# A third of the weight differences computed on GpSimd beside the modulation sums, and the gates' rows fetched through ScalarE's queue

## The chip, the core and the metric

One core of one Trainium2 chip runs the whole program. The metric is the device time of one launch in microseconds (us). Five engines work side by side and meet through semaphores: PE (TensorE, matmuls, with PEld for its weight loads), DVE (VectorE), ACT (ScalarE), POOL (GpSimd) and SP (SyncE, which here only issues transfers). Each engine takes its instructions strictly in the order in which they stand in its own queue. An instruction that waits holds up everything behind it on its engine.

## What is computed

Two layers of a diffusion trunk, for 256 latent tokens and 256 context tokens, width 1024, all in float32. The shift, scale and gate vectors ("modulation") of a layer are one long matrix-vector product of the conditioning vector with `w_ada` (1024 x 9216 for each layer).

```python
def swiglu(h, w1, w2):
    a, b = jnp.split(h @ w1, 2, axis=-1)          # 1024 -> 2 x 2816
    return (jax.nn.silu(a) * b) @ w2              # 2816 -> 1024

for layer in range(2):
    m = jnp.split(silu(c) @ w_ada[layer] + b_ada[layer], 9, axis=-1)   # and the same for the context
    x = sandwich_out(x, swiglu(sandwich_in(x, m, 0, g[0]), w1[layer, 0], w2[layer, 0]), m, 0, g[1], 0.5)
    x = sandwich_out(x, token_mixing(sandwich_in(x, m, 1, g[2]), ...), m, 1, g[3], 1.0)
    x = sandwich_out(x, swiglu(sandwich_in(x, m, 2, g[4]), w1[layer, 1], w2[layer, 1]), m, 2, g[5], 0.5)

def sandwich_in(x, mods, idx, g):       # norm, then scale and shift
    return rms_norm(x, g) * (1 + mods[3 * idx + 1]) + mods[3 * idx]
def sandwich_out(x, y, mods, idx, g, w):    # gate on the way back
    return x + w * mods[3 * idx + 2] * rms_norm(y, g)
```

There are four SwiGLU blocks ("FFN" below). The first three work on all 512 tokens, the last one on the 256 latent tokens alone.

## The kernel before

**Split products.** PE multiplies in a reduced float32 form (fp32r). To keep the precision, each operand is held as two blocks: `hi`, the value rounded to fp32r, and `lo`, the difference between the value and `hi`. A product is three matmuls: hi times hi, lo times hi, hi times lo (L92 is the line of all of them). Activations live in HH and HL, the hidden values of an FFN in nine pairs of blocks inside R.

**A weight unit.** Weights come in units of 128 x 1024 values (512 KB). The class `Unit` loads one into one of four raw buffers (raw0 to raw3) by a transfer on SP's queue (L183). Its method `parts` then makes the two blocks: ScalarE casts the raw values to `hi` (L190), and VectorE subtracts (`raw - hi`, L195) to make `lo`. Both go into a slot, one of the w or R tiles, and eight slots serve the units of an FFN in turn. The raw buffer is free for the next transfer when `lo` is done. Which engine subtracts is the unit's field `lo_eng`, V (VectorE) by default.

**Modulation beside the FFN.** While PE works on the FFN of one stage, VectorE computes modulation vectors that a later stage needs (`ada_v`): units of `w_ada` come through the same four raw buffers, and for each one VectorE does four multiply-adds of 128 x 512 (L486, L488) into two running sums in the tile sx. PE then adds the partitions up, and for a gate vector `gate_done` (L461, L462) adds a bias row, multiplies by a gain row and stores the gate to DRAM (L463, on ScalarE's queue). The bias and gain rows are fetched by `gate_rows` (L453, L454): eight transfers of 2 KB for a gate, four for each half of it, 48 in all, issued by SP among the weight units. They go into two sets of tiles, (grow, grow) and (rstd, rstd). Sixteen vectors are left for the first three FFNs, six in the first and five in each of the others; all six gates are among them.

**Order.** The kernel writes down a list of steps with planned times (`schedule`), then walks it once (`run`). At each step `run` first issues the loads that have a free buffer, then makes the parts of those units that are due: a unit is due when its first use is at most `LOOK` = 2.5 us of planned time away, or when its data should be there. The units come in the order of their first use. Behind this the recording layer may still swap neighbours in an engine's queue.

**An FFN** (`ffn`) goes through 22 columns of hidden blocks in three chunks. `pair` makes one hidden block from two units of w1, `chunk` multiplies a chunk's blocks by units of w2 and adds the result to the tile YB: ScalarE copies it for the first chunk (L683), VectorE adds it for the second (L685), and the third is the tail. The banks that these instructions empty are needed at once by the matmuls of the other half of the chunk.

Of the kernel before, what the change touches and what calls it, by code (L numbers as in the profile page):

```python
# [17 lines left out]
D = 1024  # L18
# [4 lines left out]
T = SEQ + CTX  # L23
# [56 lines left out]
def hybrid_trunk(ctx: ExitStack, tc, x, c, ctx_in, c_ctx, w_ada, b_ada, norm_g, ffn_w1, ffn_w2, w_in, w_out,  # L80
                 na_rpb, pool_w, pool_scale, diff_lambda, diff_subln_g, const, out):
    nc = tc.nc
    V, S, G = nc.vector, nc.scalar, nc.gpsimd
# [80 lines left out]
    def lo_engine(n):  # L164

        turn[0] += 1
        return G if n and turn[0] % n == 0 else V
# [63 lines left out]
    prog = []  # L231
# [40 lines left out]
    DMA_US, DMA_LAT, LOOK = 1.46, KN['dlat'], KN['look']  # L272

    def run():
        seq = []
        for i, st in enumerate(prog):
            for u in st.units:
                if u.first is None:
                    u.first = i
                    seq.append(u)  # L280
                u.last = i
        owner = {}
        for u in seq:
            if u.split:
                sl = min(u.slots, key=lambda z: owner[z].last if z in owner else -1)
                u.slot, u.prev = sl, owner.get(sl)
                owner[sl] = u
        mark = {st.mark: i for i, st in enumerate(prog) if getattr(st, "mark", None)}
        nl = ns = 0
        dma = 0.0  # L290

        ring = []

        def can_load(i):
            if nl >= len(seq) or mark.get(seq[nl].gate, -1) > i:
                return False
            if seq[nl].own is not None:
                p = seq[nl].own_prev
                return p is None or p.last < i
            if len(ring) < len(raws):  # L300
                return True
            o = ring[-len(raws)]
            return hasattr(o, "hi") if o.split else o.last < i

        def can_split(i):
            if ns >= nl:
                return False
            u = seq[ns]
            if not u.split:
                return True  # L310
            if isinstance(u.after, str) and mark[u.after] > i:
                return False
            return u.prev is None or u.prev.last < i

        for i, st in enumerate(prog):
            t = st.t - st.dur
            extra = 1
            while True:
                if can_load(i):
                    u = seq[nl]  # L320
                    if u.own is None:
                        u.load(raws[len(ring) % len(raws)])
                        ring.append(u)
                    else:
                        u.load(u.own)
                    dma = max(dma, t) + DMA_US
                    u.there = dma + DMA_LAT
                    nl += 1
                    continue
                if can_split(i):  # L330
                    u = seq[ns]
                    must = prog[u.first].t - prog[u.first].dur <= t + LOOK
                    if not u.split:
                        ns += 1
                        continue
                    if must or (u.there <= t and extra > 0):
                        u.parts(SLOTS[u.slot])
                        extra -= 0 if must else 1
                        ns += 1
                        continue  # L340
                break
            assert all(u.first > i or hasattr(u, "hi") or not u.split for u in st.units), i
            st.fn()
# [101 lines left out]
    def gate_set(h):  # L445
        return RSTD if h else (GROW[:, 1], GROW[:, 2])

    def gate_rows(l, j, h):

        bias, gain = gate_set(h)  # L450
        for v in range(2):
            rs = slice(64 * v, 64 * v + 64, 32)
            nc.sync.dma_start(out=bias[rs], in_=b_ada[l, j * D + h * T : j * D + (h + 1) * T].rearrange("(f c) -> f c", f=2))  # L453
            nc.sync.dma_start(out=gain[rs], in_=norm_g[l, 2 * (j // 3) + 1, h * T : (h + 1) * T].rearrange("(f c) -> f c", f=2))  # L454

    def gate_done(l, j, h):

# [12 lines left out]
    def ada_v(l, *js):  # L470

        st = []
        for j in js:
            for h in range(2):
                box = {}
                for q in range(4):
                    if q == 2 and j % 3 == 2:
                        st.append(Step(lambda l=l, j=j, h=h: gate_rows(l, j, h)))
                    u = Unit(w_ada[l, q * SEQ : (q + 1) * SEQ, j * D + h * T : j * D + (h + 1) * T], split=False)

                    def fn(u=u, q=q):
                        for z in range(2):
                            for v in range(2):
                                sv = sc[:, 2 * q + z, v : v + 1]
                                if q == 0 and z == 0:
                                    V.tensor_scalar(out=ACC[v], in0=u.raw[:, z, :], scalar1=sv, scalar2=None, op0=ALU.mult)  # L486
                                else:
                                    V.scalar_tensor_tensor(out=ACC[v], in0=u.raw[:, z, :], scalar=sv, in1=ACC[v], op0=ALU.mult, op1=ALU.add)  # L488

                    st.append(Step(fn, [u]))  # L490
# [123 lines left out]
    def ffn(l, f, groups, done=0):  # L614
# [4 lines left out]
        both = len(groups) == 2  # L619
        allc = ALLC if both else GROUPS[groups[0]]  # L620
        ring = tuple(range(8))

        def unit(src, lo=V):
            u = Unit(src, slots=ring, lo=lo)
            u.after = f"ffn{l}{f}"
            return u

# [11 lines left out]
        def w1_units(j):  # L639
            a, b = [lo_engine(KN["fmod"] if j < (KN["front"] if l == 0 or f == 0 else KN["lf"]) else 0) for _ in range(2)]  # L640
            return unit(w1[:, j * P : (j + 1) * P], a), unit(w1[:, DFF + j * P : DFF + (j + 1) * P], b)
# [60 lines left out]

        nf = 0 if done or not both else FRONT
        fr = [w1_units(j) for j in range(nf)]
        for j in range(nf):
            for u in fr[j]:
                u.hi_v = j < KN["hv"] if not both else j < KN["hb"] if f else j < KN["hc"]
# [73 lines left out]
        end = Step(lambda: None)  # L781
        end.mark = f"tail{l}{f}"
        body.append(end)
        for u in lu[1:]:
            u.after, u.tail = end.mark, True
        al = range(j0, j1)
        tail = {LAT: tail_of(2, lu, banks[0:2], al) + tail_of(3, lu, banks[2:4], al)}
        c0, c1 = [(banks[4:6], banks[0:2])[t] for t in range(2)]
# [536 lines left out]
    both = (LAT, CTXG)  # L1325
# [56 lines left out]
    def marked(name):  # L1382
        s = Step(lambda: None)
        s.mark = name
        return s

    f = ffn(0, 0, both, PAIRS)
    raw_u = [GTB[:, 0], GTB[:, 1], SX[:, :D]]
    w1f = ffn_w1[0, 0].rearrange("(k p) (h n) -> k p h n", p=P, h=2)
# [41 lines left out]
    for l in range(DEPTH):  # L1431
# [4 lines left out]
        for g, h in ((LAT, hl), (CTXG, hc)):  # L1436
            front[g][0].needs += h[:2]
            front[g][2].needs += h
        schedule(tail[LAT] + tail[CTXG] + [marked(f"mix{l}")] + wait_h(front[LAT], hl) + wait_h(front[CTXG], hc), hl + hc)
        f = ffn(l, 1, (LAT,) if last else both)  # L1440
        main.insert(len(main) // 2, Step(lambda l=l: gate_load(l, 1, (LAT,) if l else both)))
        if last:
# [15 lines left out]
        else:  # L1458
# [13 lines left out]
            tail = nf[2]  # L1472

    run()


# [23 lines left out]
```

## Time and profile before

| | us |
|---|---|
| three timed runs | 1788.02, 1788.70, 1781.35 |
| their median | 1788.02 |
| the profiled execution, whole time | 1785.39 |
| its span, first to last instruction | 1783.6 |
| PE busy in the span | 1731.2 (97%) |
| DVE busy | 1149.2 (64%) |
| ACT busy | 702.9 (39%) |
| POOL busy | 79.1 (4%) |

The first FFN runs from about 20 to 400 us of the span, the token mixing of layer 0 to about 690, the second FFN to 1015, the third to 1390, the mixing of layer 1 to about 1620, and the fourth FFN to the end. In the table PE's share says where to look, not how close PE is to its peak: what tells is the list of PE's waits, and how many matmuls a stretch holds. On DVE, ACT and POOL a busy time is the engine's own work; waits at the head of a queue are not in it.

### The profile page before, as it was taken

To read this page: it belongs to the slowest core of one execution; us is meant where nothing else is said; L and a number is where in the kernel's file an instruction comes from. 1 tells how busy PE (TensorE), PEld (TensorE's weight loads), DVE (VectorE), ACT (ScalarE), POOL (GpSimd) and SP (SyncE) were. 2 spreads that over 40 slices of the span, in tenths; PEclk is the share of its full clock that TensorE was granted. 3 is DMA by queue.
4 is the path that set the end of the run, shared out by engine and by line. 5 is a ranking of instruction groups with operands and counts; after the bars stand their busy time and mean duration, and the time that the engine had idled before them with its cause. 6 is when DMAs were issued, how large, how long until landed. Compare 5 with 4: busy or idle time off the path is not lost.

```text
span 1783.6 us, 23841 instructions
## 1 busy us (share of the span) xinstructions
PE 1731.2 (97%) x9281; PEld 1438.0 (81%) x9281; DVE 1149.2 (64%) x1804; ACT 702.9 (39%) x1224; POOL 79.1 (4%) x130
## 2 busy tenths in 40 slices
PE   6899999999999999999999999999999999979998
PEld 3687787778977789788788798888887898768997
DVE  4757767766368774666766576576765647865553
ACT  4323222235377753332222452233123536754442
POOL 0000000001000410000000000000000100300000
PEclk9999999999999999999999999999999999989999
DMA  9737546645111232565655434555555331337661
GB/s 283 226 118 215 175 143 197 180 133 137 55 53 48 85 95 84 158 197 155 188 154 165 128 109 153 154 154 177 166 153 164 98 92 60 110 116 227 185 189 60
DMA packets 292096, 255.96 MB, mean 144 GB/s; under 512 B 16128, under 2 KB 236048, under 8 KB 291984
## 3 DMA queue, kind: packets, MB, share of 16 engines
q1 hardware_dynamic: 290176, 253.48, 47.7%
q8 instruction: 72, 1.18, 0.3%
q10 hardware_dynamic: 1808, 0.97, 0.2%
q14 instruction: 40, 0.33, 0.1%
HBM read 253.32 MB, written 1.10 MB: 143 GB/s over the span
## 4 chain that ended last, share of the span: by engine, by line
PE 80%; DMA 8%; DVE 6%; ACT 4%; issue 2%; SPq 0%; ACTq 0%; POOL 0%; DVEq 0%; POOLq 0%
PE bank L92 78%; DMA raw<-in_ffn_w_dram 6%; DVE R L195 1%; DVE sx L488 1%; ACT R L190 1%; PE bank L882 1%; DVE w L195 1%; ACT w L190 1%; PE bank L560 1%; DMA raw<-in_w_ada_dram 1%; DMA gtb<-in_w_ada_dram 1%; ACT YB L867 0%; DMA sil<-in_b_ada_dram 0%; DVE R L376 0%; DVE sil L634 0%
## 5 line engine op out<-in xcount | busy, mean ns | idle before, releaser
L92 PE MATMUL bank<-HH,R 128*128 128x512 f32 (+1 forms) x1932 | 511.4, 349 | 4.6 <-ACT HH L1362 3.5
L92 PE MATMUL bank<-HH,w 128*128 128x512 f32 (+1 forms) x1508 | 424.2, 360 | 0.0
L92 PEld LDWEIGHTS bank<-HH,R 128*128 128x128 f32 x1932 | 339.8, 190 | 56.6 <-issue 6.6
L92 PE MATMUL bank<-R 128*128 128x512 f32 (+3 forms) x1728 | 380.1, 377 | 2.2 <-ACT R L1101 0.9
L92 PEld LDWEIGHTS bank<-R 128*128 128x128 f32 (+1 forms) x1728 | 293.0, 188 | 73.0 <-issue 6.7
L92 PE MATMUL bank<-HL,R 128*128 128x512 f32 (+1 forms) x966 | 334.6, 346 | 0.0
L195 DVE TENSOR_TENSOR R<-raw,R 128x1024 fp32r<-128x1024 f32 (+1 forms) x182 | 221.0, 1219 | 151.4 <-ACT R L190 151.1
L488 DVE SCALAR_TENSOR_TENSOR sx<-raw,sc,sx 128x512 f32<-128x512 f32 x448 | 309.9, 747 | 12.9 <-DMA raw<-in_w_ada_dram 12.7
L190 ACT CAST R<-raw 128x1024 fp32r<-128x1024 f32 (+1 forms) x182 | 189.3, 1045 | 317.4 <-DMA raw<-in_ffn_w_dram 221.1
L92 PEld LDWEIGHTS bank<-HH,w 128*128 128x128 f32 x1508 | 268.2, 190 | 47.6 <-issue 9.6
L195 DVE TENSOR_TENSOR w<-raw,w 128x1024 fp32r<-128x1024 f32 (+1 forms) x140 | 171.4, 1226 | 152.0 <-ACT w L190 150.3
L92 PE MATMUL bank<-HL,w 128*128 128x512 f32 (+1 forms) x754 | 268.3, 356 | 0.0
L190 ACT CAST w<-raw 128x1024 fp32r<-128x1024 f32 (+1 forms) x140 | 146.1, 1047 | 233.5 <-DMA raw<-in_ffn_w_dram 160.5
L92 PE MATMUL bank<-w,R 128*128 128x512 f32 x864 | 210.5, 394 | 6.2 <-DVE YB L685 2.2
L92 PEld LDWEIGHTS bank<-HL,R 128*128 128x128 f32 x966 | 183.2, 190 | 22.5 <-DVE HL L1363 0.2
L92 PEld LDWEIGHTS bank<-w,R 128*128 128x128 f32 x864 | 159.5, 188 | 43.8 <-issue 3.2
L92 PEld LDWEIGHTS bank<-HL,w 128*128 128x128 f32 x754 | 143.2, 190 | 19.1 <-issue 0.7
L636 ACT CAST R<-sil 128x512 fp32r<-128x512 f32 (+1 forms) x92 | 49.7, 540 | 158.5 <-DVE sil L634 158.3
L634 DVE TENSOR_TENSOR sil<-sil,bank 128x512 f32<-128x512 f32 (+1 forms) x92 | 53.9, 586 | 89.2 <-PE bank L92 88.8
L530 POOL TENSOR_TENSOR sr<-sr,eps 128x1 f32<-128x1 f32 x42 | 29.0, 692 | 1426.0 <-DVE sr L529 1426.0
L633 ACT ACTIVATE sil<-bank 128x512 f32<-128x512 f32 (+1 forms) x92 | 47.4, 516 | 81.4 <-PE bank L92 77.5
L637 DVE TENSOR_TENSOR R<-sil,R 128x512 fp32r<-128x512 f32 (+1 forms) x92 | 54.2, 590 | 18.4 <-ACT R L636 18.0
(163 smaller groups left out, 1245.6 us busy)
## 6 DMA issues: line engine op xcount, KB each, us to landing
raw<-in_ffn_w_dram SPq DMA_DIRECT2D x258, 512.0 KB
raw<-in_w_ada_dram SPq DMA_DIRECT2D x128, 512.0 KB
raw<-in_w_in_dram SPq DMA_DIRECT2D x40, 512.0 KB
raw<-in_w_out_dram SPq DMA_DIRECT2D x16, 512.0 KB
gtb<-in_w_ada_dram SPq DMA_DIRECT2D x20, 256.0 KB
gtb<-gate SPq DMA_DIRECT2D x10, 512.0 KB
raw<-in_ffn_w_dram SPq DMA_DIRECT2D x8, 384.0 KB
sx<-in_w_ada_dram SPq DMA_DIRECT2D x8, 256.0 KB
```

The lines of the kernel that those rows point to most:

```text
L92: tab["mm"] = nc.tensor.matmul(out=o, lhsT=l, rhs=r, start=start, stop=stop)
L190: ins = S.copy(out=self.hi, in_=self.raw)
L195: ins = self.lo_eng.tensor_tensor(out=self.lo, in0=self.raw, in1=self.hi.bitcast(F32), op=ALU.subtract)
L488: V.scalar_tensor_tensor(out=ACC[v], in0=u.raw[:, z, :], scalar=sv, in1=ACC[v], op0=ALU.mult, op1=ALU.add)
L530: G.tensor_tensor(out=a, in0=a, in1=mhalf, op=ALU.pow)
L560: ins = nc.tensor.transpose(out=pt[:, z, t * P : (t + 1) * P], in_=y[:, t, k * P : (k + 1) * P], identity=ident)
L633: S.activation(out=sl[:, cs], in_=oa, func=AF.Silu)
L634: V.tensor_tensor(out=sl[:, cs], in0=sl[:, cs], in1=ob, op=ALU.mult)
L636: tab["hs"] = S.copy(out=uh[:, cs], in_=sl[:, cs])
L637: tab["hv"] = V.tensor_tensor(out=ul[:, cs], in0=sl[:, cs], in1=uh[:, cs].bitcast(F32), op=ALU.subtract)
L882: nc.tensor.transpose(out=bv[:, n, i * P : (i + 1) * P], in_=e[:, i * nk + n * P : i * nk + (n + 1) * P], identity=ident)
```

## The change

Four edits. (1) In `ffn`, `unit` counts its calls, and in the three FFNs that work on all tokens every third unit gets `lo_eng = G`: GpSimd does its subtraction. (2) The units of the first four columns of an FFN, whose subtraction stands at the hand-over from the stage before, and those of the tail are set back to VectorE. (3) In `run` a unit of GpSimd is due 3.5 us of planned time earlier than the others. (4) `gate_rows` issues its transfers on ScalarE's queue in place of SP's.

```diff
@@ run @@
-                    must = prog[u.first].t - prog[u.first].dur <= t + LOOK
+                    must = prog[u.first].t - prog[u.first].dur <= t + LOOK + (3.5 if u.lo_eng is G else 0.0)
@@ gate_rows @@
-            nc.sync.dma_start(out=bias[rs], in_=b_ada[l, j * D + h * T : j * D + (h + 1) * T].rearrange("(f c) -> f c", f=2))
-            nc.sync.dma_start(out=gain[rs], in_=norm_g[l, 2 * (j // 3) + 1, h * T : (h + 1) * T].rearrange("(f c) -> f c", f=2))
+            nc.scalar.dma_start(out=bias[rs], in_=b_ada[l, j * D + h * T : j * D + (h + 1) * T].rearrange("(f c) -> f c", f=2))
+            nc.scalar.dma_start(out=gain[rs], in_=norm_g[l, 2 * (j // 3) + 1, h * T : (h + 1) * T].rearrange("(f c) -> f c", f=2))
@@ ffn @@
+        asked = [0]
 
         def unit(src, lo=V):
             u = Unit(src, slots=ring, lo=lo)
+            asked[0] += 1
+            if both and asked[0] % 3 == 0:
+                u.lo_eng = G
             u.after = f"ffn{l}{f}"
             return u
@@ ffn, the first four columns @@
         fr = [w1_units(j) for j in range(nf)]
+        for u in sum(fr, ()):
+            u.lo_eng = V
@@ ffn, the tail @@
         for u in lu[1:]:
-            u.after, u.tail = end.mark, True
+            u.after, u.tail, u.lo_eng = end.mark, True, V
```

What this makes of the engines' queues, at three places. On POOL, between the square roots of the start (L530) and those of the end of the first FFN, before:

```order
L530 TENSOR_TENSOR sr_83<-sr_83,eps 128x1 x2
L530 TENSOR_TENSOR sr_84<-sr_84,eps 128x1 x2
L530 TENSOR_TENSOR sr_85<-sr_85,eps 128x1 x2
L530 TENSOR_TENSOR sr_86<-sr_86,eps 128x1 x2
L905 MEMSET YB 128x384
```

and with the change:

```order
L530 TENSOR_TENSOR sr_84<-sr_84,eps 128x1 x2
L195 TENSOR_TENSOR w_74<-raw_68,w_74 128x1024
L195 TENSOR_TENSOR R<-raw_71,R 128x1024
L195 TENSOR_TENSOR w_72<-raw_68,w_72 128x1024
L195 TENSOR_TENSOR R<-raw_68,R 128x1024
L195 TENSOR_TENSOR R<-raw_70,R 128x1024
L195 TENSOR_TENSOR w_73<-raw_70,w_73 128x1024
```

Seventeen subtractions stand between the two pairs of square roots in the first FFN, and seventeen in each of the next two: 51 of the 322 that VectorE did.

On DVE, late in the first FFN (about 243 to 258 us of the span before; R and w are slots, raw_68 to raw_71 the four raw buffers, sx the running sums), before:

```order
L195 TENSOR_TENSOR R<-raw_69,R 128x1024
L488 SCALAR_TENSOR_TENSOR sx<-raw_68,sc,sx 128x512 x2
L195 TENSOR_TENSOR w_72<-raw_71,w_72 128x1024
L195 TENSOR_TENSOR w_73<-raw_69,w_73 128x1024
L634 TENSOR_TENSOR sil_75<-sil_75,bank_102 128x512
L637 TENSOR_TENSOR R<-sil_75,R 128x512
L195 TENSOR_TENSOR R<-raw_69,R 128x1024
L486 TENSOR_SCALAR sx<-raw_70,sc 128x512 x2
```

and with the change (line numbers of the changed file, six or four higher behind the edits):

```order
L195 TENSOR_TENSOR R<-raw_69,R 128x1024
L195 TENSOR_TENSOR w_73<-raw_69,w_73 128x1024
L638 TENSOR_TENSOR sil_75<-sil_75,bank_102 128x512
L641 TENSOR_TENSOR R<-sil_75,R 128x512
L486 TENSOR_SCALAR sx<-raw_70,sc 128x512 x2
```

Two subtractions have left VectorE's queue here, the one into w_72 and the second one into R. A multiply-add on raw_68 has moved by a place, and the rest stands as it stood.

On ACT, at the start (junk and sr are the sums of squares of the first norm, L1322; the copies to rows, L1339, carry the first modulation sums on to PE), before:

```order
L1322 ACTIVATE junk,sr_83<-X 128x512
L1312 ACTIVATE sil_75<-sil_75 16x128
L1322 ACTIVATE junk,sr_83<-X 128x512 x3
L1339 COPY rows<-bank_105 128x256
L1322 ACTIVATE junk,sr_84<-X 128x512 x4
L190 CAST w_72<-raw_70 128x768
```

and with the change:

```order
L1328 ACTIVATE junk,sr_83<-X 128x512
L453 DMA grow<-in_b_ada_dram 2x256
L1328 ACTIVATE junk,sr_83<-X 128x512
L454 DMA grow<-in_norm_g_dram 2x256
L1328 ACTIVATE junk,sr_83<-X 128x512
L453 DMA grow<-in_b_ada_dram 2x256
L454 DMA grow<-in_norm_g_dram 2x256
L453 DMA rstd_91<-in_b_ada_dram 2x256
L454 DMA rstd_92<-in_norm_g_dram 2x256
L453 DMA rstd_91<-in_b_ada_dram 2x256
L1345 COPY rows<-bank_105 128x256
L454 DMA rstd_92<-in_norm_g_dram 2x256
```

The eight row transfers of the first gate now stand around the first copy to rows. On SP they stood behind the start, among the weight units of the first FFN. The casts L190 keep their places among ScalarE's other instructions, but for some swaps of neighbours.

## Rows read from the trace of the kernel before

**Rows 1.** The page's first part: busy time, share of the span, instructions.

```profile
PE 1731.2 (97%) x9281; PEld 1438.0 (81%) x9281; DVE 1149.2 (64%) x1804; ACT 702.9 (39%) x1224; POOL 79.1 (4%) x130
```

**Rows 2.** Windows: stretch and length, busy us (instructions) per engine, clock, DMA.

```profile
56.00:58.00 2.00, 1.72 (x5) 1.43 (x6) 1.60 (x3) 0.50 (x2) 0.00 (x0) 0.54 1.06 350
...
200.00:250.00 50.00, 50.00 (x232) 40.11 (x231) 32.76 (x55) 10.91 (x15) 0.00 (x0) 1.00 0.49 150
...
750.00:800.00 50.00, 48.10 (x222) 38.30 (x221) 28.59 (x38) 17.00 (x23) 0.00 (x0) 1.00 0.65 185
```

**Rows 3.** PE's waits: instruction, what ended the wait, us in total, times, longest.

```profile
PE bank L92 <- ACT HH L1362: 3.5, 1, 3.5
...
PE bank L92 <- DVE YB L685: 2.2, 2, 1.8
PE bank L92 <- ACT YB L683: 2.1, 2, 1.9
...
PE bank L92 <- DVE s L1361: 1.1, 1, 1.1
...
PE bank L92 <- ACT w L190: 1.1, 1, 1.1
```

**Rows 4.** The page's groups: VectorE's subtractions, mean ns, idle before them and why.

```profile
L195 DVE TENSOR_TENSOR R<-raw,R 128x1024 fp32r<-128x1024 f32 (+1 forms) x182 | 221.0, 1219 | 151.4 <-ACT R L190 151.1
...
L195 DVE TENSOR_TENSOR w<-raw,w 128x1024 fp32r<-128x1024 f32 (+1 forms) x140 | 171.4, 1226 | 152.0 <-ACT w L190 150.3
```

**Rows 5.** Timeline of POOL in the first mixing: start, duration, instruction.

```profile
588.24 1.25 POOL L945 TENSOR_TENSOR YB<-YB,cst 128x8 f32<-128x8 f32 x1
...
591.06 0.73 POOL L949 TENSOR_TENSOR sx<-YB 128x256 f32<-128x256 f32 x1
591.86 2.24 POOL L930 TENSOR_TENSOR YB<-YB 128x271 f32<-128x271 f32 x2
...
594.83 0.20 POOL L945 TENSOR_TENSOR YB<-YB,cst 128x8 f32<-128x8 f32 x1
```

**Rows 6.** Timeline of DVE at the same place.

```profile
591.16 1.71 DVE L195 TENSOR_TENSOR R<-raw,R 128x1024 fp32r<-128x1024 f32 x1 [0.34 <-ACT R L190]
```

**Rows 7.** Timelines of DVE and PE: a subtraction and its first use.

```profile
971.47 1.22 DVE L195 TENSOR_TENSOR w<-raw,w 128x1024 fp32r<-128x1024 f32 x1
...
976.81 0.62 PE L92 MATMUL bank<-HH,w 128*128 128x512 f32 x2
```

**Rows 8.** Timelines of DVE, SP and PE around a chunk's end in the second FFN.

```profile
744.27 0.69 DVE L637 TENSOR_TENSOR R<-sil,R 128x512 fp32r<-128x512 f32 x1
744.87 0.75 DVE L488 SCALAR_TENSOR_TENSOR sx<-raw,sc,sx 128x512 f32<-128x512 f32 x1
745.53 1.22 DVE L195 TENSOR_TENSOR w<-raw,w 128x1024 fp32r<-128x1024 f32 x1
746.67 2.07 DVE L488 SCALAR_TENSOR_TENSOR sx<-raw,sc,sx 128x512 f32<-128x512 f32 x3
748.65 1.22 DVE L195 TENSOR_TENSOR R<-raw,R 128x1024 fp32r<-128x1024 f32 x1
...
748.77 7.63 SPq L183 DMA_DIRECT2D raw<-in_ffn_w_dram  x3
...
756.97 2.37 PE L92 MATMUL bank<-w,R 128*128 128x512 f32 x9 [1.90 <-ACT YB L683]
```

**Rows 9.** Issues by line: count, ns (min/median/max), first and last start.

```profile
L453 SPq DMA_DIRECT2D grow<-in_b_ada_dram x12: 472/481/606, 60.9 to 1170.4; - x12
...
L463 ACTq DMA_DIRECT2D gate<-grow x12: 487/498/618, 119.3 to 1362.7; - x12
```

**Rows 10.** Timelines of ACT, DVE and PE in the start.

```profile
11.96 0.37 ACT L1339 COPY rows<-bank 128x256 f32<-128x256 f32 x1 [3.78 <-PE bank L92]
...
16.17 0.75 DVE L1323 TENSOR_SCALAR YB<-X,sr 128x1024 f32<-128x1024 f32 x1 [0.66 <-POOL sr L530]
...
21.38 1.06 PE L1359 MATMUL bank<-cst,YB 128*128 128x128 f32 x4
```

## The prediction, made before the changed kernel ran

> **What bounds the kernel now.** I read the busy shares first, then the matmul count in windows, then PE's waits. PE is busy for 97% of the span [rows 1]. That alone proves little, so the windows matter: a 50 us stretch in the middle of an FFN holds 232 matmuls at the full granted clock [rows 2], one in 0.216 us, and the stretch with the worst wait among the bodies of the first three FFNs still holds 222 [rows 2]. So there PE runs without gaps nearly everywhere. The list of its waits says how much is left [rows 3]: in the bodies of these FFNs, where the change works, PE waits 2.2 us for additions into YB on VectorE (L685) and 2.1 us for copies into YB on ScalarE (L683); at a tail there is one wait of 1.1 us for a cast. In the start it waits 3.5 us for a cast to HH and 1.1 us for VectorE's s. All five together are 10.0 us, 0.56% of the span. The change takes nothing out of PE's own work. So its gain can be no more than about these 10 us, while a loss has no such ceiling. VectorE, at 64% [rows 1], is no bound; it is idle for 303 us ahead of its 322 subtractions, nearly all of it waiting for ScalarE's cast [rows 4].
>
> **The subtractions themselves.** 51 of 322 leave VectorE. At 1.22 us each [rows 4] that is 62 us of its busy time, all of it beside PE's work. On GpSimd such a subtraction does not occur in the trace. The nearest rows are a two-input instruction over 256 columns, 0.73 us, and one over 8 columns, 0.20 us [rows 5]: (0.73 - 0.20) / 248 = 2.1 ns a column, so an estimate of 0.20 + 1016 x 0.00214 = 2.4 us for 1024 columns. The bounds are 1.22 us, VectorE's own time, and 4 x 0.73 = 2.9 us. I take 2.4, since the two short rows already show how the time grows with the columns. Who waits for it? I followed each of the 51 units from the end of its subtraction to the first matmul that reads it. The smallest distance is 4.12 us: the subtraction that begins at 971.47 and takes 1.22, read at 976.81 [rows 7]. The other fifty lie between 4.6 and 38 us, with a median of about 15. A subtraction that takes 1.2 us more, and starts up to 1.2 us later behind one of VectorE's, ends before its use everywhere. **Price at PE: 0.**
>
> **What GpSimd's work does to VectorE.** In the mixing the two engines run side by side, and the rows show that they take turns. VectorE's subtraction at 591.16 took 1.71 us in place of 1.22 while GpSimd's instruction of 591.06 ran until 591.79 [rows 5, 6]; in return, two additions on GpSimd that follow at 591.86 took 2.24 us together, and an instruction of 8 columns took 1.25 us at 588.24 against 0.20 at 594.83 [rows 5]. So each engine's two-input instruction waits until the other's is over. VectorE gets back about 1.14 us for each subtraction moved (the spacing of its starts, 745.53 to 746.67 [rows 8]) and may lose 2.4 us of standing still. Over 51 units that is between -58 us and +64 us of VectorE's time, in an engine with 36% to spare. PE sees it only where VectorE is late already.
>
> The Trainium skill states the same as a rule against this kind of change: in "SBUF — State Buffer", section "Who interferes with whom", a VectorE instruction with two SBUF inputs and a GpSimd instruction that reads SBUF exclude each other, and the second to issue blocks fully until the first is over. By that rule VectorE stands still whenever it has such work, and the sum would be the slower rival's below; the trace agrees on the mechanism (1.71 us against 1.22), while how often the two meet in an FFN no row of this case shows.
>
> **Where VectorE is late already.** Three places in the three bodies carry waits for emptied banks of more than 0.3 us: two of VectorE's (2.2 us in all) and one of ScalarE's (1.90 of its 2.1).
> - At 757 us PE waits 1.90 us for ScalarE's copy [rows 8]. That copy stands behind casts whose loads SP issued from 748.77 on, as the raw buffers came free. Ahead of this VectorE works without a gap from 744.27 to 749.88, and two of its subtractions there, 745.53 and 748.65, go to GpSimd [rows 8]. They give back 2 x 1.14 = 2.3 us and may block 2 x 2.4 = 4.8 us, since every other instruction in this stretch has two SBUF inputs. So between -1.9 (the wait goes) and +2.5. I take +2, because here VectorE has work queued at every moment.
> - At 275 us the 1.8 us wait [rows 3] stands behind a subtraction that stays on VectorE, whose load came late. The one two units ahead goes to GpSimd. Between -1.8 and +1.2; I take -0.5.
> - At 888 us it is 0.4 us. I take 0.
>
> **Sum for the bodies: +1.5 us, between -4 and +4.**
>
> **The start.** The first unit for GpSimd is the one whose late cast makes PE wait 3.5 us [rows 3]. The cast stays where it is, so the wait stays, and with it the lower clock behind it: 0.54 granted in the 2 us after PE stood still, between the levels of 1.2 and 2.4 GHz [rows 2]. The difference HL for the next matmuls has two SBUF inputs and now meets GpSimd's first subtraction, up to 2.4 us minus the 1.14 that VectorE saves. Against that, one transpose for a later block moves ahead in PE's queue, which can save the 1.1 us wait for s [rows 3], while four of the next block move behind eighteen matmuls. I take +0.5, between -1.1 and +3.
>
> **The row transfers.** SP loses 48 issues of 0.48 us, 23 us; ScalarE gains 48 of about 0.50, the time that its own issue of a gate takes [rows 9], 24 us in an engine that is 39% busy [rows 1]. What queues behind them: casts and the silu of the next hidden block. Each batch of four waits for VectorE's two instructions of the gate before; ScalarE already waits for the second of them at L463, a few instructions later, so little is new. In the start eight issues, 8 x 0.50 = 4.0 us, stand around the first copy to rows, where ScalarE is idle for 3.78 us [rows 10], and one of them waits for the landing of an earlier one. If ScalarE comes 2 us late there, the norm's YB, done at 16.92, comes 2 us later and is read by PE at 21.38 [rows 10]: 4.5 us of cover. **Price: 0**; were the cover gone, up to +4. SP's gain is worth nothing by itself, since its loads wait for raw buffers, which come free by the subtractions.
>
> **The longer look-ahead** moves next to nothing: in ScalarE's queue the casts keep their places but for swaps of neighbours, since most units are made as soon as their data is there. 0.
>
> **The sum.** 1785.4 + 0 + 1.5 + 0.5 + 0 + 0 = 1787.4 us against the profiled execution, 0.1% more. That execution lies 2.6 us under the median of the three runs, which themselves spread over 7 us; so I say **1788.0**, no change. What a measurement of this kernel can tell from no change is about 0.5%, 9 us.
>
> **Rivals.**
> 1. *Faster, VectorE's queue is freed.* A subtraction on VectorE waits at the head of its queue for a cast, and the modulation sums behind it wait too: 303 us of idle time for 322 units [rows 4], so some 48 us for 51. With these on GpSimd the sums go on, raw buffers come free sooner, loads start sooner, and PE's waits for late loads and late copies go. For it speaks the size of this idle time; against it, that ScalarE's casts still stand in one queue, and that PE has only 10.0 us of waits to give [rows 3]. If all go: 1785.4 - 10.0 = 1775.4 us.
> 2. *Slower, VectorE and GpSimd block each other.* It decides where loads run just ahead of their use: about 231 to 275, 680 to 757 and 850 to 888 us, which hold 11 of the 51 units. If each blocks VectorE for its whole length, raw buffers come free 11 x (2.4 - 1.14) = 14 us later in all, and PE gets it in full: 1799 us. For it, [rows 5, 6] and the gapless stretch of [rows 8]; against it, VectorE's idle time and the distances of 4.12 us and more. It takes over once a subtraction on GpSimd ends more than 1.22 + 4.12 = 5.3 us after its cast.
> 3. *Slower, ScalarE is held up by the rows.* Each batch of four costs it 2.0 us, ahead of a silu or a cast. If six of the twelve batches fall on a chunk's end, where PE waits for ScalarE's copies, 6 x 2.0 = 12 us: 1797 us. Against it: of twelve chunk halves' ends only three show a wait of over 0.3 us today.
> That the change doesn't do what it says is no rival: the queues hold 51 subtractions on POOL and 48 row transfers on ACT.
>
> **Chances.** No change, within 9 us of the median: 0.73. Rival 1, faster by more: 0.10. Rival 2: 0.12 and rival 3: 0.05, together slower 0.17. The range takes in the bounds above and part of the rivals: from 1778.5 (rival 1 nearly whole) to 1799 (rival 2).
>
> **What would show it.** The forecast: POOL's subtractions at about 2.4 us, some of them 3 to 4; VectorE's two-input rows stretched beside them; VectorE's busy time down by less than 62 us; PE's matmul count in 200 to 250 us still 232, and its waits for YB within 2 us of today's. Rival 1: those waits gone, and less idle time ahead of L195 by far more than 48 us. Rival 2: new PE waits on POOL's R and w, or longer ones at the chunk ends. Rival 3: ACT's queue waiting at L453 and L454 just ahead of copies to YB, or the start's transposes at 21.38 later. I am wrong if a subtraction on GpSimd takes over 5 us, or if PE's waits outside the start and the three bodies change.

## The result, and the profile with the change

The change is slower: 1812.3 us (median of four runs, 1810.3 to 1814.9) against 1787.6, a ratio of 1.0151 with a 95% interval of 1.0136 to 1.0166, so 24 to 30 us. The prediction, 1788.0 with a range up to 1799.0, is wrong. The profiled execution took 1810.75 us, its span is 1809.0 against 1783.6. Its first line answers to [rows 1]:

```profile
PE 1741.4 (96%) x9281; PEld 1442.7 (80%) x9281; DVE 1146.2 (63%) x1753; ACT 701.1 (39%) x1224; POOL 212.7 (12%) x181
```

VectorE has 51 instructions fewer and is as busy as before: 1146.2 us against 1149.2. The groups by line, which answer to [rows 4], say why (busy us, mean ns of one, idle before and its cause):

```profile
L488 DVE SCALAR_TENSOR_TENSOR sx<-raw,sc,sx 128x512 f32<-128x512 f32 x448 | 343.3, 822 | 26.5 <-DMA raw<-in_w_ada_dram 26.3
L195 DVE TENSOR_TENSOR R<-raw,R 128x1024 fp32r<-128x1024 f32 (+1 forms) x152 | 188.0, 1241 | 140.1 <-ACT R L190 139.5
L195 DVE TENSOR_TENSOR w<-raw,w 128x1024 fp32r<-128x1024 f32 (+1 forms) x119 | 148.9, 1253 | 147.9 <-ACT w L190 146.7 <-ACT YB L873 0.9
```

The 51 subtractions were worth 51 x 1.22 = 62 us to VectorE, and its other instructions grew by 59, that is 1.16 us for each one moved. The multiply-adds of the modulation alone take 343.3 us; in the trace of before the same 448 took 309.9.

PE's waits, which answer to [rows 3] (what ended the wait, us in total, times, longest; L687 and L689 are L683 and L685 of before, L1368 is L1362; the 6.4 us at L1320, in the start, stand in place of one wait of 7.2 us for the constants at the same line, L1314, before):

```profile
PE bank L92 <- ACT YB L687: 8.7, 2, 4.4
...
PE bank L92 <- DMA gtb<-in_w_ada_dram: 7.9, 3, 6.8
PE bank L92 <- DVE YB L689: 7.3, 4, 3.7
PE bank L1320 <- ACT junk L1328: 6.4, 1, 6.4
...
PE bank L92 <- ACT HH L1368: 2.7, 1, 2.7
...
PE bank L92 <- POOL w L195: 1.7, 1, 1.7
```

The waits for emptied banks (YB) went from 4.3 to 16.0 us. I matched PE's matmuls of the two traces in their order; the distance between equal matmuls grows at six places and hardly anywhere else. The first matmul of the first FFN comes 2.9 us later (27.95 against 25.01); by 90 us 1.9 of this are left. Then the distance grows by 5.6 us about 142 us of the old span, by 2.9 about 275, by 4.1 about 757, by 2.9 about 976 and by 6.9 about 1265; between and behind these it moves by less than 2 us. In the end it is 25.4 us. Four of the five places in the bodies are ends of chunks 0 and 1, where PE needs its banks emptied. At 142 the kernel before waited 0.22 us, and at 1265 not at all.

### The profile page after: what moved, and what is told of

Its sections match the earlier page's. It is cut to its first block, busy times and chain, and to the rows that moved or that the text cites. A ratio compares the mean times of both kernels' runs of the same rounds, so it can differ in the third digit from the quotient of the medians.

```text
span 1809.0 us, 23921 instructions
## 1 busy us (share of the span) xinstructions
PE 1741.4 (96%) x9281; PEld 1442.7 (80%) x9281; DVE 1146.2 (63%) x1753; ACT 701.1 (39%) x1224; POOL 212.7 (12%) x181
## 4 chain that ended last, share of the span: by engine, by line
PE 70%; DMA 11%; DVE 9%; ACT 4%; issue 3%; POOL 2%; SPq 0%; ACTq 0%; DVEq 0%; POOLq 0%
PE bank L92 68%; DMA raw<-in_ffn_w_dram 9%; DVE sx L488 3%; ACT R L190 2%; DVE R L195 1%; ACT w L190 1%; DVE w L195 1%; POOL R L195 1%; PE bank L888 1%; PE bank L560 1%; POOL w L195 1%; DMA raw<-in_w_ada_dram 1%; DMA gtb<-in_w_ada_dram 1%; DVE sx L486 1%; DVE sil L638 0%
## 5 line engine op out<-in xcount | busy, mean ns | idle before, releaser
L488 DVE SCALAR_TENSOR_TENSOR sx<-raw,sc,sx 128x512 f32<-128x512 f32 x448 | 343.3, 822 | 26.5 <-DMA raw<-in_w_ada_dram 26.3
L190 ACT CAST R<-raw 128x1024 fp32r<-128x1024 f32 (+1 forms) x182 | 189.2, 1045 | 333.5 <-DMA raw<-in_ffn_w_dram 246.7
L195 DVE TENSOR_TENSOR R<-raw,R 128x1024 fp32r<-128x1024 f32 (+1 forms) x152 | 188.0, 1241 | 140.1 <-ACT R L190 139.5
L195 DVE TENSOR_TENSOR w<-raw,w 128x1024 fp32r<-128x1024 f32 (+1 forms) x119 | 148.9, 1253 | 147.9 <-ACT w L190 146.7
L190 ACT CAST w<-raw 128x1024 fp32r<-128x1024 f32 (+1 forms) x140 | 146.1, 1046 | 246.1 <-DMA raw<-in_ffn_w_dram 167.2
L92 PE MATMUL bank<-w,R 128*128 128x512 f32 x864 | 218.2, 403 | 14.0 <-DVE YB L689 7.3
L92 PEld LDWEIGHTS bank<-w,R 128*128 128x128 f32 x864 | 163.5, 193 | 55.2 <-DVE YB L689 9.0
L195 POOL TENSOR_TENSOR R<-raw,R 128x1024 fp32r<-128x1024 f32 x30 | 80.1, 2670 | 519.7 <-ACT R L190 429.6
L530 POOL TENSOR_TENSOR sr<-sr,eps 128x1 f32<-128x1 f32 x42 | 30.2, 720 | 497.2 <-DVE sr L529 497.2
L195 POOL TENSOR_TENSOR w<-raw,w 128x1024 fp32r<-128x1024 f32 x21 | 52.4, 2495 | 301.1 <-ACT w L190 276.7
```

The lines of the kernel that those rows point to most:

```text
L92: tab["mm"] = nc.tensor.matmul(out=o, lhsT=l, rhs=r, start=start, stop=stop)
L190: ins = S.copy(out=self.hi, in_=self.raw)
L195: ins = self.lo_eng.tensor_tensor(out=self.lo, in0=self.raw, in1=self.hi.bitcast(F32), op=ALU.subtract)
L530: G.tensor_tensor(out=a, in0=a, in1=mhalf, op=ALU.pow)
```

## How a late raw buffer reaches PE

The timeline about the first of these places, 148 us of the new span: rows of POOL, DVE, SP, ACT and PE put in order of time, the others left out (start, length, instruction, in brackets the idle time before it and what ended it).

```profile
122.03 2.68 POOL L195 TENSOR_TENSOR R<-raw,R 128x1024 fp32r<-128x1024 f32 x1 [29.68 <-ACT R L190]
122.36 2.90 DVE L488 SCALAR_TENSOR_TENSOR sx<-raw,sc,sx 128x512 f32<-128x512 f32 x1
125.29 0.37 SPq L183 DMA_DIRECT2D raw<-in_w_ada_dram  x1
125.75 3.03 SPq L183 DMA_DIRECT2D raw<-in_ffn_w_dram  x2
127.17 1.21 DVE L195 TENSOR_TENSOR w<-raw,w 128x1024 fp32r<-128x1024 f32 x1
132.72 1.05 ACT L190 CAST R<-raw 128x1024 fp32r<-128x1024 f32 x1 [3.08 <-DMA raw<-in_ffn_w_dram]
133.85 2.40 POOL L195 TENSOR_TENSOR R<-raw,R 128x1024 fp32r<-128x1024 f32 x1 [9.13 <-ACT R L190]
134.75 2.58 DVE L195 TENSOR_TENSOR w<-raw,w 128x1024 fp32r<-128x1024 f32 x1 [4.39 <-ACT w L190]
136.27 1.45 SPq L183 DMA_DIRECT2D raw<-in_ffn_w_dram  x2
140.45 1.05 ACT L190 CAST R<-raw 128x1024 fp32r<-128x1024 f32 x1 [5.73 <-DMA raw<-in_ffn_w_dram]
141.53 1.23 DVE L195 TENSOR_TENSOR R<-raw,R 128x1024 fp32r<-128x1024 f32 x1 [4.21 <-ACT R L190]
142.79 0.37 SPq L183 DMA_DIRECT2D raw<-in_ffn_w_dram  x1
146.81 1.04 ACT L190 CAST R<-raw 128x1024 fp32r<-128x1024 f32 x1 [5.03 <-DMA raw<-in_ffn_w_dram]
147.76 0.58 ACT L687 COPY YB<-bank 128x512 f32<-128x512 f32 x1
148.39 1.90 PE L92 MATMUL bank<-R 128*128 128x512 f32 x4 [4.28 <-ACT YB L687]
```

Read it from top to bottom. GpSimd's subtraction holds the multiply-add on VectorE for 2.90 us (0.75 alone). SP issues its next two loads only when these two instructions let go of their raw buffers. The third load has to wait for VectorE's subtraction of 127.17, which stands behind the held multiply-add; it is issued at 128.41 (the second of the two in the row of 125.75) and brings the cast of 132.72. GpSimd subtracts for that block until 136.25, and VectorE's subtraction of 134.75, which meets it, takes 2.58 us. The next load starts at 136.27, and its block is cast at 140.45, subtracted until 142.76, and its buffer loaded again from 142.79. ScalarE sits idle for 5.03 us for this last load, because the cast that needs it stands in its queue **ahead of the copy into YB**. PE has been waiting for this copy for 4.28 us. The block being cast is not what PE needs next. So at this place a late raw buffer costs PE nothing by its own block's lateness; it costs where a cast, or a subtraction on VectorE, stands ahead of the instructions that empty PE's banks.

The granted clock adds to it. Windows of the changed kernel (stretch, length, busy us and instructions of PE, PEld, DVE, ACT, POOL, clock, DMA share, GB/s), and below them two of the kernel before, behind its own waits of 1.8 and 1.9 us:

```profile
148.00:150.00 2.00, 1.61 (x4) 1.32 (x5) 2.00 (x3) 2.00 (x5) 0.00 (x0) 0.66 0.56 158
150.00:152.00 2.00, 2.00 (x6) 1.54 (x5) 2.00 (x4) 0.74 (x1) 0.00 (x0) 0.50 0.65 210
...
1286.00:1292.00 6.00, 6.00 (x14) 4.70 (x15) 1.65 (x3) 1.04 (x1) 1.70 (x1) 0.50 0.30 87
```

```profile
275.00:277.00 2.00, 1.59 (x7) 1.33 (x8) 1.55 (x3) 0.40 (x1) 0.00 (x0) 1.00 0.68 191
...
757.00:759.00 2.00, 2.00 (x9) 1.63 (x10) 0.69 (x1) 0.40 (x1) 0.00 (x0) 1.00 0.87 247
```

Behind these waits of 1.8 and 1.9 us the clock stayed at 2.4 GHz; behind 4.3 and 3.7 us it stood at half of that, 1.2 GHz. From 1286 to 1292 PE did 14 matmuls in 6 us; at 0.216 us [rows 2] these are 3.0 us of work, so the lower clock cost 3.0 us there, nearly as much as the wait of 3.7. Over the span the mean granted clock is 0.989, against 0.995 before: 0.011 x 1809 less 0.005 x 1784 is an estimate of 11 us of lost clock, some of which falls into the waits.

## Experiments

Each is compared with the kernel before on the same chip. The diffs show the lines that matter; those that pick the units or add a field, and `gate_rows` put back on SP, are left out, and @@ marks a jump. **Which edit is it?** The first three runs undo parts.

### The rows alone

The fourth edit alone, in both lines of `gate_rows`:

```diff
-            nc.sync.dma_start(out=bias[rs], in_=b_ada[l, j * D + h * T : j * D + (h + 1) * T].rearrange("(f c) -> f c", f=2))
+            nc.scalar.dma_start(out=bias[rs], in_=b_ada[l, j * D + h * T : j * D + (h + 1) * T].rearrange("(f c) -> f c", f=2))
```

> The fourth edit alone: the gates' rows come on ScalarE's queue, all subtractions stay on VectorE. Theory: the rows cost only in the start, where eight small transfers come between SP's first loads and make it wait for other transfers to land; PE's wait for gtb is about 6.8 us as in the changed kernel (4.4 before), its first transposes wait for a late sum of squares, and the whole kernel is 2 to 3 us slower, 1789 to 1791, with the chunk ends of the FFNs as before (waits for copies and additions into YB within 1 us of 2.1 and 2.2). Rival, that ScalarE held up by the rows makes the chunk ends late: 1797 or more, with the waits for YB at 8.7 and 7.3 us as in the changed kernel.

Measured: 1785.47 us against 1783.92, a ratio of 1.0007 [0.9998, 1.0016]. This can't be told from no change, and it is under the 2 to 3 us of the theory; the rival is out. The trace shows the mechanism all the same. Equal matmuls stand 1.6 to 1.9 us later from the start up to 258 us, PE's longest wait for gtb is 6.5 us (6.8 with the whole change, 4.2 to 4.4 in every run with the rows on SP), and the waits for YB are 2.4 us (L683) and one gap of 0.8 (L685). SP's waits in the first 30 us:

```profile
SPq L208 <- DMA X<-in_ctx_dram: 2.3, 1, 2.3
...
SPq L1301 <- DMA grow<-in_b_ada_dram: 1.2, 1, 1.2
```

Neither stands in the trace of before. SP and ScalarE take the completion semaphores of their transfers from one set of eight in turn, as the kernel's waits show, and a transfer first waits until the one eight before it has landed. Eight small transfers in the start bring SP's first weight loads nearer to the transfers ahead of them: with this edit a load of w1 (L208) waits for context tokens to land (X) that SP itself asked for just ahead of it.

### The third on GpSimd alone, with and without the longer look-ahead

Edits 1 to 3 with `gate_rows` on SP; then the same with

```diff
-                    must = prog[u.first].t - prog[u.first].dur <= t + LOOK + (3.5 if u.lo_eng is G else 0.0)
+                    must = prog[u.first].t - prog[u.first].dur <= t + LOOK
```

> Edits 1 to 3 alone: GpSimd takes its third with the longer look-ahead, the rows stay on SP's queue. Theory: the loss in the FFN bodies is the subtractions', so it stays: 1807 to 1811, PE waiting at the chunk ends near 142, 275, 757 and 1265 us of the kernel before for copies and additions into YB, and the start as before (HH wait 3.5). Rival, that the rows on ScalarE make the chunk ends late: under 1797.

> Edits 1 and 2 alone: rows on SP, and the units of GpSimd due at the same 2.5 us as the others. Theory (the look-ahead moves next to nothing): within 4 us of the run with edits 1 to 3, 1808 to 1815. Rival, that casts made 3.5 us earlier stand in the way of copies on ScalarE: under 1803.

Measured: 1812.32 us, ratio 1.0160 [1.0143, 1.0176], and 1815.05 us, ratio 1.0158 [1.0139, 1.0177]. So the subtractions make the whole loss, and the look-ahead none of it. In the first of the two, PE's waits for YB are these:

```profile
PE bank L92 <- ACT YB L687: 12.4, 3, 5.2
...
PE bank L92 <- DVE YB L689: 6.5, 3, 3.1
```

**What of a subtraction on GpSimd is it?** Three runs change one property each.

### GpSimd's part cut to 8 columns

```diff
+            w = 8 if self.lo_eng is G and self.asked else self.nk * self.n
-            ins = self.lo_eng.tensor_tensor(out=self.lo, in0=self.raw, in1=self.hi.bitcast(F32), op=ALU.subtract)
+            lo, raw, hi = [z.rearrange("p k n -> p (k n)")[:, :w] for z in (self.lo, self.raw, self.hi)]
+            ins = self.lo_eng.tensor_tensor(out=lo, in0=raw, in1=hi.bitcast(F32), op=ALU.subtract)
```

> Edits 1 to 3, but the GpSimd subtractions (49 of 51; two in the first FFN stay on VectorE whole) cover 8 of 1024 columns; the rest of these lo blocks is left as it was. So VectorE is freed of 49 subtractions, the order and the look-ahead are those of edits 1 to 3, and GpSimd is done 0.2 us after the cast. Theory: the loss comes from the length of GpSimd's work, so it is gone: 1779 to 1788, no chunk-end gap over 2 us. Rival, that the new order or the look-ahead makes the loss: 1800 or more. That VectorE's freed queue was worth something (the prediction's first rival) would show as under 1780.

Measured: 1781.39 us against 1783.92, ratio 0.9988 [0.9978, 0.9999]. The first line of its page:

```profile
PE 1736.1 (97%) x9281; PEld 1441.5 (81%) x9281; DVE 1095.4 (61%) x1757; ACT 702.4 (39%) x1224; POOL 98.9 (6%) x177
```

The trace holds 47 of these short subtractions, not 49. Edit 2 finds no first columns to set back in the first FFN, so the first twelve units there, which this run leaves to VectorE, hold four of GpSimd's and not two. VectorE is busy for 54 us less than before, and no wait for copies or additions into YB at a chunk's end over 0.4 us is left. The order of the queues is thus not the cause, and 54 us of VectorE's time are worth 2 us to PE. More the change could hardly have brought.

### Blocking alone

VectorE does all subtractions; at the same units GpSimd subtracts the hi block from itself into a scratch tile (`hi` stands for the flattened view of the slot's first half):

```diff
+            if self.asked:
+                G.tensor_tensor(out=IDLE, in0=hi, in1=hi, op=ALU.subtract)
```

> Before's subtractions all on VectorE and its look-ahead, and on GpSimd, at the same 51 units, a subtraction of the same 128 x 1024 form that reads the hi block twice and writes a scratch tile that nobody reads. No raw buffer waits for GpSimd itself; only VectorE can be held up. Theory (GpSimd blocks VectorE, and so the raw buffers come free late): slower by 12 to 30 us, VectorE's rows at 2.4 to 3.7 us beside GpSimd's, gaps at the chunk ends. Rival, that the loss is only GpSimd's own 2.4 to 2.7 us in place of VectorE's 1.22 before the raw buffer is free: within 3 us of before.

Measured: 1797.95 us, ratio 1.0077 [1.0061, 1.0092], +14 us. The first line of its page:

```profile
PE 1737.7 (97%) x9281; PEld 1440.9 (80%) x9281; DVE 1201.6 (67%) x1804; ACT 701.7 (39%) x1224; POOL 219.3 (12%) x181
```

VectorE, with the same instructions as before, is busy for 52 us longer: 1.03 us for each of the 51. PE's waits for YB are 12.7 us. So blocking VectorE is enough to make the kernel slower, but only by half of the loss.

The Trainium skill has the rule ("SBUF — State Buffer", section "Who interferes with whom"): whoever of VectorE with two SBUF inputs and GpSimd reading SBUF issues first makes the other stand still to its end. The rows agree: 2.90 us for 0.75 beside GpSimd's 2.68.

### Short, but the raw buffer held

As with 8 columns, at the same 47 units, and behind each a transfer of 4 KB out of the raw buffer:

```diff
+            if w == 8:
+                behind(nc.gpsimd.dma_start(out=held, in_=self.raw[:, 0, 0:8]), ins)
```

> As the run with 8 of 1024 columns (the same 49 lo blocks are left as they were), and behind each of these short subtractions GpSimd sends 4 KB of the raw buffer to a scratch place in DRAM, so that the raw buffer stays taken for about 2 us longer, with no long instruction on GpSimd. Theory A (two parts: VectorE blocked, worth the 14 us of the run with blocking alone, and the raw buffer taken longer, worth about as much): slower by 5 to 18 us, 1789 to 1802. Rival B, that only VectorE's blocking counts: as the run with 8 columns, within 3 us of 1781.

Measured: 1796.78 us, ratio 1.0058 [1.0043, 1.0073], against 0.9988 without the transfers: 0.70%, 12.5 us, from nothing but buffers that stay taken. The line view of the transfers gives the time to landing:

```profile
DMA to landing us min/median/max: 1.7/2.7/5.6
```

So a buffer is taken some 3 us longer than with 8 columns alone. (GpSimd's transfers count on semaphores of their own, so SP's loads do not wait for them as in the first run.) VectorE is busy for 1094.8 us and not blocked, and yet PE's waits at the chunk ends are there:

```profile
PE bank L92 <- DVE YB L695: 5.9, 3, 3.0
PE bank L92 <- ACT YB L693: 5.1, 2, 4.4
```

Rival B falls. In the change it is GpSimd's own 2.6 us in place of 1.22 that hold the buffer, 1.4 us longer and not 3. An estimate from these runs doesn't add up to the 28 us: -2 for VectorE's freed time, +14 for blocking, and for the buffer 12.5 x (2.6 - 1.2) / 3 = 6 by proportion, make 18. That the rest comes from both meeting at the same chunk ends was not tried.

### Four pieces

Each of GpSimd's subtractions as four instructions of 256 columns:

```diff
+            for c in range(4 if self.lo_eng is G and self.asked else 1):
+                w = self.nk * self.n // (4 if self.lo_eng is G and self.asked else 1)
+                lo, raw, hi = [z.rearrange("p k n -> p (k n)")[:, c * w : (c + 1) * w] for z in (self.lo, self.raw, self.hi)]
```

> Edits 1 to 3 with the rows on SP, and each subtraction on GpSimd in four pieces of 256 columns. If VectorE is held up for one instruction of GpSimd at a time, it now gets in between after some 0.7 us, while GpSimd's unit takes longer where VectorE is busy: VectorE's longest instructions fall from 2.9 to about 1.5 us, the sum stays, and the time is 1800 to 1812. If the two took no turns but shared, the pieces would change nothing in VectorE's rows.

Measured: 1840.47 us, ratio 1.0301 [1.0286, 1.0316], twice the loss. GpSimd's groups:

```profile
L199 POOL TENSOR_TENSOR R<-raw,R 128x256 fp32r<-128x256 f32 x120 | 117.8, 1011 | 503.9 <-ACT R L191 489.7 <-DMA raw<-in_ffn_w_dram 8.3 <-issue 5.8
L199 POOL TENSOR_TENSOR w<-raw,w 128x256 fp32r<-128x256 f32 x84 | 72.7, 896 | 292.3 <-ACT w L191 260.1 <-DVE sx L492 18.9 <-PE bank L92 13.4
```

A piece takes 1011 or 896 ns where 0.73 would do alone [rows 5]: now GpSimd stands still between its pieces. From the first piece to the end of the fourth a unit takes 3.74 us in the mean and up to 6.4, against 2.60. VectorE does lose less (busy 1127.8 us against 1144.9 uncut, of 1087 without any blocking), but the raw buffer is taken longer, and the kernel loses more. No run separates the two here. My expectation missed it, since it counted VectorE's side alone.

### Away from the chunk ends

Only units of five columns behind each chunk's end, 24 in place of 51:

```diff
@@ ffn, unit @@
-            if both and asked[0] % 3 == 0:
+            if both and far[0] and asked[0] % 3 == 0:
@@ ffn, the columns of a chunk @@
+                far[0] = ci > 0 and j - lo < 5
```

> Edits 1 to 3 with the rows on SP, but only units of the first five columns behind a chunk's end are asked for, 24 in place of 51, so none whose raw buffer is needed for the last loads ahead of a chunk's end. Theory (late raw buffers make the last casts ahead of a chunk's end late, and the copies and additions into YB stand behind these): no PE gap over 2 us at a chunk's end, within 4 us of before, 1780 to 1788. Rival, that each subtraction on GpSimd costs its share wherever it stands: 24/51 of 28, 13 us slower.

Measured: 1795.02 us, ratio 1.0045 [1.0028, 1.0062], +8 us. This lies between the two, and the run is no clean test: units are loaded and cast well ahead of their use (the prediction found a median of 15 us and up to 38), so one of these "behind" chunk 0 was subtracted ahead of its end, at 116.84 us in the first FFN and at 750.03 in the second. The gaps followed at 141.85 (2.0 us, 0.2 before) and 763.09 (2.5 us, 1.9 before). Ahead of the first gap GpSimd had done this one subtraction only:

```profile
116.84 2.70 POOL L195 TENSOR_TENSOR R<-raw,R 128x1024 fp32r<-128x1024 f32 x1 [100.60 <-ACT R L190]
149.13 2.47 POOL L195 TENSOR_TENSOR w<-raw,w 128x1024 fp32r<-128x1024 f32 x1 [29.58 <-ACT w L190]
```

**Why does PE see it?** The last two runs change the order at a chunk's end alone.

### Copies first, with GpSimd's third and without

```diff
@@ parts @@
+            if "holdv" in tab and self.lo_eng is V:
+                behind(ins, tab["holdv"])
@@ run @@
-                    if must or (u.there <= t and extra > 0):
+                    if must or (u.there <= t and extra > 0 and not st.quiet):
@@ ffn, chunk @@
-                                        S.copy(out=ys, in_=o)
+                                        tab["hold"] = S.copy(out=ys, in_=o)
-                                        V.tensor_tensor(out=ys, in0=o, in1=ys, op=ALU.add)
+                                        tab["holdv"] = V.tensor_tensor(out=ys, in0=o, in1=ys, op=ALU.add)
+                        st[-1].quiet = j + 2 == j1
```

`tab["hold"]` is what `parts` already looks at for the casts.

> Edits 1 to 3 with the rows on SP, and one more: at a chunk's end the copies and additions into YB stand ahead of the casts and subtractions of units that are used later (no unit that is not due is made in the steps of a chunk's last weight unit, and the casts and VectorE's subtractions recorded behind a copy or an addition may not be moved ahead of it). GpSimd's work and VectorE's blocking stay. Theory (PE waits because its copies stand behind casts whose loads are late, not because its own weights are late): the gaps of 2 to 5 us at the chunk ends fall under 1 us, and most of the 28 us goes, 1782 to 1796. Rival, that the weights themselves are late: PE's waits move from YB to L190 and L195, and the time stays over 1803.

> The kernel before with the same rule for the order at a chunk's end, and nothing else. Theory: its own gaps of 1.8 us near 275 and 1.9 us near 757 go, 1780 to 1786, 0.1 to 0.3% faster than before. Rival, that the casts now come late for the next columns: no gain or slower, with new waits for L190.

Measured: with GpSimd's third 1787.80 us, ratio 1.0019 [1.0010, 1.0029]; without it 1780.58 us, ratio 0.9974 [0.9965, 0.9983]. GpSimd's third, which cost 28 us in the old order, costs 7 in this one. POOL and VectorE are as busy as in the changed kernel (215.1 and 1146.1 us): the blocking and the longer hold are all still there. ScalarE's timeline at the end of chunk 0 with GpSimd's third:

```profile
137.86 1.95 ACT L689 COPY YB<-bank 128x512 f32<-128x512 f32 x3
139.71 2.00 ACT L190 CAST R<-raw 128x1024 fp32r<-128x1024 f32 x2
...
147.33 1.05 ACT L190 CAST R<-raw 128x1024 fp32r<-128x1024 f32 x1 [5.62 <-DMA raw<-in_ffn_w_dram]
```

A cast still waits 5.62 us for its load, but the copies are over by then, and nobody at PE waits. Of the waits for these copies and additions one of 1.8 us is left (near 273), and behind it the granted clock fell:

```profile
272.00:274.00 2.00, 1.36 (x4) 1.07 (x5) 2.00 (x4) 0.00 (x0) 0.00 (x0) 0.71 0.77 245
274.00:276.00 2.00, 2.00 (x6) 1.57 (x5) 0.91 (x2) 1.04 (x1) 0.00 (x0) 0.50 0.67 227
```

About the third FFN's chunk 1 it is 1.00. So the theory holds but for this one gap, and the rival, that the weights themselves are late, falls. The kernel before with this order has no wait left at a chunk's end: its distance to the old order falls by 2.1 us near 275 and by 2.2 near 757, where the two waits stood. It is the fastest of all, 4.9 us under the kernel before and some 32 us under the changed one. (Single traces differ too: by 30 us of the span PE is 2.8 us ahead here, where the queues of both kernels are still the same.)

## Why the prediction was wrong

- **What bounds the kernel.** Right as far as the runs go: no run gained more than 5 us, and 54 us of VectorE's time are worth 2.
- **GpSimd's subtraction, 2.4 us.** Right: the shortest took 2.37 us, the median is 2.40, and the mean 2.60 with those that stood still.
- **Turn-taking on VectorE.** The bounds were right, 1.14 us back and up to 2.4 lost: of the 1.22 that each took along 1.16 were lost again, so next to nothing came back.
- **"PE sees it only where VectorE is late already."** This is the step that failed. I took a PE wait in the trace of before for the sign of such a place. But the wait shows only where the margin is used up already, and I did not work out how much was left elsewhere. At 142 us there was a wait of 0.22 us, which I had left out as too short, and so no margin at all; at 1265 us there was no wait and a margin of half a microsecond. These two places lost 5.6 and 6.9 us, half of the loss. The sum for the bodies was +1.5 us, between -4 and +4; it is +22. The two lines of the kernel before, PE's first matmul behind the copy at 142 us and, at 1265, VectorE's first addition, which ends at 1264.63 us for a matmul that PE starts at 1265.12:

```profile
142.43 0.50 PE L92 MATMUL bank<-R 128*128 128x512 f32 x1 [0.22 <-ACT YB L683]
...
1263.95 0.68 DVE L685 TENSOR_TENSOR YB<-bank,YB 128x512 f32<-128x512 f32 x1
```

- **The sizes at the named places.** At 757 us I took +2 of at most 2.5; it was 4.1. At 275 us I took -0.5 of at most +1.2; it was 2.9. Both were bounded by the length of one or two blocked instructions. A late buffer passes its lateness on through the next load, cast and subtraction, and the wait is followed by a stretch at half the clock; I had the lower clock in [rows 2] and priced it in the start only.
- **"Price at PE: 0" for the block's own use.** Wrong by one unit, the one of 4.12 us that I had named. Its subtraction ran from 991.54 to 993.91 us and PE waited 1.7 us for it. GpSimd's extra length is 1.15 us of this wait; it reaches PE only because the cast came some 5 us later against PE than before, behind a late load. I had moved the subtraction and held the cast still.
- **The start, +0.5, and the row transfers, 0 with a cover of 4.5 us.** With the whole change PE is 1.9 us late by 90 us. The rows move the start by 1.6 to 1.9 us in the run with them alone, while that run's time can't be told from no change. I looked at ScalarE's 0.5 us an issue and at the norm, and not at the transfers of SP that wait for transfers to land. With the rows on SP the start came no later than before.
- **The look-ahead, 0.** Right.
- **The rivals.** Rival 2 was half of the right mechanism, with a chance of 0.12: it had VectorE blocked, and not the raw buffer that GpSimd itself holds longer. Its 14 us were the sum of one buffer's delay each, over the stretches with visible waits; the losses near 142, 976 and 1265 us lay outside them. That the run with blocking alone measured +14 too is luck: part of its loss, 4.2 us, lies near 1265. Its "new PE waits on POOL's R and w, or longer ones at the chunk ends" is what the trace shows. Rival 3 is ruled out by the run with the rows alone, rival 1 by the one with 8 columns.

## What to carry to other kernels

Before work is moved to an engine that is slower or shares with a busy one, ask who waits for the buffer it holds, and follow the lateness through one whole turn: release, load, cast, and then what stands behind that cast in its queue. A place without a wait in the old trace is not a place with margin; the margin has to be read, as the distance between the end of the instruction that empties the bank and PE's next need. And where a cheap copy that PE waits for stands behind a cast of something used much later, put it ahead: here it took away 21 of 28 us, and 4.9 us from the kernel before.

## What was not expected of the hardware

Cutting GpSimd's instruction in four to let VectorE in between doubled the loss (1.030 against 1.016): the pieces stood still as well, 3.74 us a unit in place of 2.60. And a wait of PE can be dearer than its length: behind 3.7 us the granted clock was 0.50 for the next 6 us, which cost another 3.0 us. The length alone doesn't tell: behind 1.8 and 1.9 us in the kernel before it stayed at 1.00, behind 1.8 us with the copies first it fell. The run away from the chunk ends has both: 0.50 behind its wait of 2.0 us (at 141.85), 1.00 behind a longer one of 2.3 us (at 277.2).

```profile
144.00:146.00 2.00, 2.00 (x6) 1.63 (x5) 2.00 (x4) 0.20 (x1) 0.00 (x0) 0.50 0.66 188
277.00:279.00 2.00, 1.83 (x8) 1.53 (x9) 1.31 (x3) 0.48 (x1) 0.00 (x0) 1.00 0.75 219
```
